# Cutting the first heads' weight products into three spans of rows, with four heads ahead and a rearranged opening

## The chip, the cores and the metric

One Trainium2 chip, one core of it. The metric is the device time of one execution in microseconds (us), as the median of the runs shown; lower is better. Each kernel also has one profiled execution, and the trace that is read below is that one's. TensorE (PE) multiplies, VectorE (DVE), ScalarE (ACT) and GpSimd (POOL) work element by element, SyncE's queue (SP) issues the loads.

## The reference, cut to what matters

Two layers on 256 tokens of 2048 channels, in float32. Each layer has a token mixer and a SwiGLU block; in front of each stands a norm whose scale and shift come from a conditioning vector `c`.

```python
c_act = silu(c)
for i in range(2):
    sh1, sc1, g1, sh2, sc2, g2 = split(c_act @ w_mod[i] + b_mod[i], 6)
    h = rms_norm(x, norm1_g[i]) * (1 + sc1) + sh1
    y = retention_mixer(h, cos, sin, ...) if i == 0 else short_conv_mixer(h, ...)
    x = x + g1 * y
    h = rms_norm(x, norm2_g[i]) * (1 + sc2) + sh2
    x = x + g2 * swiglu(h, ...)
return rms_norm(x, final_g)
```

The retention mixer has eight heads. Each needs, of `h @ w_in`, 256 columns of queries, 256 of keys, 512 of values and 512 of gates. Queries and keys are turned by an angle (position times a frequency, through sine and cosine), their scores are weighted by a decay, multiplied with the values, normed, and multiplied with silu of the gates.

## The kernel before, in words

**Layout.** `x` is kept transposed: 16 rows (tiles) of 128 channels x 256 tokens. A *unit* is the product of one 128 x 128 block of weights with one row. To keep float32's precision, weights and rows are each split into a high part and the rest (`hi`, `lo`; `h[k][:, 0]`, `h[k][:, 1]`), and a unit is three matmuls of 256 columns (`packed`, L348 to L366: hi x high at L361, hi x low at L362, lo x high at L363) or one of 512 and one of 256 (`product`, L328, lines L338 and L341).

**Weights.** All weights lie in one array in the order of use (`in_use_order`, `laid_out`), in blocks of 1 MB, one load each. `prepare` (L282) takes half of such a block (128 x 1024, eight units): ACT casts the high part (L295), DVE subtracts it from the raw weights (L296). `take` (L301) hands out the next unit's weights, and prepares when none is ready; from `early` units on it holds `AHEAD` = 2 more halves ready.

**Modulation.** Scale, shift and gate are made one column of 128 channels at a time (`modulation`, L232): a load of 1 MB of `w_mod`, one DVE instruction that multiplies 128 x 2048 with silu of `c` and sums (L238), and one or two operations on a column on POOL (L243, L245, L248). Those of the first norm are made in the opening, all others beside later products, at points that `plan_mod` (L257) gives in units done; the first are due from `early` - 64 = 376 units on.

**Opening.** Loads of `c`, `x`, the columns and a table (frequencies and identity) are issued first (L194 to L222). The 16 squares go to ACT one by one, DVE adds them (L384 to L388), PE sums the one tile over partitions (L396), DVE makes the mean (L405), POOL the root (L407), PE spreads it (L414) and ACT copies it to `rb` (L577). Then `row(k)` makes row k of `h`: DVE multiplies x with the scale and `rb` (`u`, L424), ACT adds the shift for the high part (L431), DVE makes the low part (L432). Each row needs two modulation columns first.

**First heads.** The products of heads 0 and 1 (queries, keys, gates: 16 columns in eight PSUM banks, all that there are) run row by row as the rows are made, for rows 0 to 10 (`RET_FIRST`, `FIRST_KS` = 11; L592). The banks are copied to SBUF (`held`, L565) as `ahead`. Then the angles are worked out (L595, L529 to L561: 19 operations on DVE, two sines on ACT). Then rows 0 to 10 of heads 2, 3 and 4 are multiplied pair by pair of columns (`RET_SECOND`, L598 to L603), while rows 11 to 15 are made. After that the heads come one by one (`projections`, L714): `pair` (L704) multiplies the five late rows for heads 0 to 4 and adds what was held (L711), `rope` turns queries and keys, `values` (L627; L634 to L636) multiplies all 16 rows, `scores` (L646; first matmul L656, split at L378), two more `pair`s for the gates, and the rest of the head (`mixed`, L670) is done in steps among later products (`asides`, `STEPS`). 460 units stand ahead of head 0's values: 16 x 11 + 24 x 11, and 2 x 2 x 5 for its queries and keys.

**Order.** PE runs in the order in which the program is written (`manual_schedule`, L188), through the whole kernel. DVE and ACT are in written order only within the opening (L588); elsewhere the framework's scheduler orders them. Tile pools set when a buffer comes free: three raw tiles for the weights, three for the opening's modulations (`START_RAWS`), four high and four low parts.

Of the kernel before, what the change touches and what calls it, by code (L numbers as in the profile page):

```python
# [33 lines left out]
FIRST_KS = 11  # L34
EARLY_HEADS = 5
START_RAWS = 3
# [19 lines left out]
class Group:  # L56
    """Output columns of a matrix that are worked out together, in the order of their rows."""
# [29 lines left out]
def out_groups(rows, parts, tail, lead):  # L87
    """The first columns' products with the last rows, which are made last, come after the others."""
# [21 lines left out]
RET_FIRST, RET_SECOND, RET_HEADS = ret_in_groups()  # L110
# [7 lines left out]
def in_use_order():  # L118
    """Each group of the weights, with its matrix and the matrix's index, in the order of use."""
    yield "ret_w_in", 0, RET_FIRST  # L120
    for groups in RET_SECOND:
        for g in groups:
            yield "ret_w_in", 0, g
# [19 lines left out]
def laid_out(arrays):  # L143
    """The weights in the order of their use, as blocks of 128 rows and CHUNK columns."""
# [27 lines left out]
def trunk(ctx: ExitStack, tc: tile.TileContext, x_in, c_in, pos_in, w_mod, cols_in, tab_in, w_all, out):  # L172
# [21 lines left out]
    with tc.tile_pool(name="crow", bufs=1) as cp:  # L194
        row = cp.tile([1, D], F32, tag="row", name="row")
        nc.sync.dma_start(row, c_in)
        for i in range(0, D, 2 * S):
            pt = ps.tile([P, 2, S], F32, tag="bank", name=name("bank")).rearrange("p a b -> p (a b)")
            nc.tensor.matmul(pt, ones[0:1, :], row[:, i : i + 2 * S], start=True, stop=True)
            nc.scalar.activation(cb[:, i : i + 2 * S], pt, AF.Silu)  # L200
    x = []
    for i in range(0, KT, 4):
        t = const.tile([P, 4, S], F32, tag=f"x{i}", name=f"x{i}")
        nc.sync.dma_start(t, x_in[:, i : i + 4, :])
        x += [t[:, j, :] for j in range(4)]
    n_cols = cols_in.shape[1]
    cols = const.tile([P, n_cols], F32, tag="cols", name="cols")
    nc.sync.dma_start(cols, cols_in)
# [13 lines left out]
    nc.sync.dma_start(tab, tab_in[:, : 1 + P])  # L222
# [9 lines left out]
    def modulation(layer, which, j, pool=wpool, bufs=RAW_BUFS):  # L232
        t = layer * 6 * KT + which * KT + j
        raw = pool.tile([P, CHUNK], F32, tag="raw", name=name("raw"), bufs=bufs)
        nc.sync.dma_start(raw, w_mod[t])
        total = tmp("msum", (P, 1), bufs=4)
# [289 lines left out]
    with ExitStack() as inner:  # L526
# [322 lines left out]
```

## Time and profile before

| | us |
|---|---|
| runs: lowest, median, highest of 3 | 2663.68, 2667.03, 2669.86 |
| profiled execution, span from first to last instruction | 2660.6 |
| PE busy in the span | 2621.9 |
| DVE, ACT, POOL busy in the span | 2017.8, 1248.4, 214.0 |
| PE busy from 0 to 31 / 31 to 104 / 104 to 120 / 120 to 211 | 14.1 / 63.7 / 15.5 / 91.0 |
| DVE busy in the same four stretches | 18.8 / 72.8 / 15.9 / 65.4 |
| mean rate of loads and stores over the span | 258 GB/s |

Rows of the trace in time order give the start and the duration (us), the engine, the line, the operation, what is written and read, and the shape; in brackets stands how long the engine waited before and for what. PEld is PE's loading of weights, SPq the issue of a load on SP's queue. Rows of the waits give the waiting instruction, what ended the wait, the sum, the number and the longest. Rows of windows give for a stretch the busy time and count of PE, PEld, DVE, ACT and POOL, then the granted TensorE clock (1.00 is full), the load engines' busy share and GB/s. Rows of groups give busy time and mean ns of one, then the idle time before them and what ended it. "x4" at the end of a row counts the instructions that it stands for.

### The profile page before, as it was taken

What the parts mean: (1) busy time and instruction counts of PE and PEld (TensorE: products, weight loads), DVE (VectorE), ACT (ScalarE), POOL (GpSimd) and SP (SyncE); (2) the same over time, 40 slices, a digit from 0 to 9 for tenths busy, and PEclk for the clock granted to TensorE, in tenths of its full rate; (3) what the DMA queues carried; (4) which work ended last, traced back from release to release, by engine and by line L of the source; (5) the groups of instructions that cost most, each with busy time, mean ns of one, the idle gap of its engine ahead of it and who ended that gap; (6) DMA issues with size and microseconds to landing.
All of it is one profiled execution on the core that took longest, in us unless ns stands there. A gap on an engine that the chain in (4) does not pass through costs nothing.

```text
span 2660.6 us, 40134 instructions
## 1 busy us (share of the span) xinstructions
PE 2621.9 (99%) x16044; PEld 2335.6 (88%) x16044; DVE 2017.8 (76%) x2655; ACT 1248.4 (47%) x1782; POOL 214.0 (8%) x278
## 2 busy tenths in 40 slices
PE   6999999999999999999999999999999999999998
PEld 5898988999989888888888898888998888888887
DVE  8968988887698877777777889878887665555554
ACT  3444543444456444334444454444554443444443
POOL 4310000011000010100000001100000000000000
PEclk9999999999999999999999999999999999999999
DMA  9976667777677877777777768776777765555553
GB/s 374 400 265 242 251 217 296 267 270 263 250 267 261 312 281 267 298 271 284 285 268 282 268 219 321 287 282 256 268 269 256 264 220 190 185 185 189 189 190 127
DMA packets 96957, 687.69 MB, mean 258 GB/s; under 512 B 10753, under 2 KB 12545, under 8 KB 13825
## 3 DMA queue, kind: packets, MB, share of 16 engines
q1 hardware_dynamic: 96770, 685.13, 69.3%
q8 instruction: 125, 2.05, 0.3%
q14 instruction: 62, 0.51, 0.1%
HBM read 682.99 MB, written 2.10 MB: 257 GB/s over the span
## 4 chain that ended last, share of the span: by engine, by line
PE 76%; issue 19%; DVE 3%; DMA 0%; POOL 0%; ACT 0%; DVEq 0%; ACTq 0%; POOLq 0%
PE bank L338 35%; PE bank L341 18%; PE bank L363 4%; PE bank L361 4%; PE bank L362 4%; PE bank L634 2%; PE bank L635 2%; PE bank L636 2%; PE bank L477 1%; PE bank L476 1%; PE bank L478 1%; DVE raw L238 1%; DVE lo L296 1%; PE bank L680 0%; DMA raw<-w_mod 0%
## 5 line engine op out<-in xcount | busy, mean ns | idle before, releaser
L296 DVE TENSOR_TENSOR lo<-raw,hi 128x1024 fp32r<-128x1024 f32 x912 | 1113.5, 1223 | 561.1 <-ACT hi L295 559.2
L295 ACT CAST hi<-raw 128x1024 fp32r<-128x1024 f32 x912 | 953.9, 1050 | 1087.3 <-PE bank L338 638.5
L338 PE MATMUL bank<-h,hi 128*128 128x512 f32 x3296 | 1155.2, 395 | 0.0
L341 PE MATMUL bank<-h,lo 128*128 128x256 f32 x3296 | 925.5, 281 | 0.0
L338 PEld LDWEIGHTS bank<-h,hi 128*128 128x128 f32 x3296 | 622.7, 189 | 144.9
L338 PE MATMUL bank<-mid,hi 128*128 128x512 f32 x2100 | 731.1, 395 | 0.1
L341 PEld LDWEIGHTS bank<-h,lo 128*128 128x128 f32 x3296 | 623.3, 189 | 0.0
L341 PE MATMUL bank<-mid,lo 128*128 128x256 f32 x2100 | 583.8, 278 | 0.0
L338 PEld LDWEIGHTS bank<-mid,hi 128*128 128x128 f32 x2100 | 394.1, 188 | 92.2 <-DVE mid L378 0.4
L238 DVE SCALAR_TENSOR_TENSOR raw<-raw,cb 128x2048 f32<-128x2048 f32 x192 | 438.5, 2284 | 5.0 <-DMA raw<-w_mod 4.8
L341 PEld LDWEIGHTS bank<-mid,lo 128*128 128x128 f32 x2100 | 395.0, 188 | 0.0
L363 PE MATMUL bank<-h,lo 128*128 128x256 f32 x1024 | 292.4, 286 | 10.0 <-DVE lo L296 10.0
L361 PE MATMUL bank<-h,hi 128*128 128x256 f32 x1024 | 290.6, 284 | 2.8 <-ACT hi L295 2.8
L362 PE MATMUL bank<-h,hi 128*128 128x256 f32 x1024 | 290.3, 284 | 0.6 <-DVE h L432 0.5
L363 PEld LDWEIGHTS bank<-h,lo 128*128 128x128 f32 x1024 | 193.8, 189 | 14.4 <-DVE lo L296 14.4
L361 PEld LDWEIGHTS bank<-h,hi 128*128 128x128 f32 x1024 | 195.7, 191 | 3.5 <-ACT hi L295 3.3
L362 PEld LDWEIGHTS bank<-h,hi 128*128 128x128 f32 x1024 | 193.9, 189 | 2.3 <-DVE h L432 2.3
L243 POOL TENSOR_SCALAR mcol<-msum,cols 128x1 f32<-128x1 f32 x64 | 63.6, 994 | 549.6 <-DVE raw L238 549.6
L634 PE MATMUL bank<-hi,h 128*128 128x512 f32 x256 | 101.4, 396 | 0.0
L635 PE MATMUL bank<-lo,h 128*128 128x512 f32 x256 | 101.0, 395 | 0.0
L636 PE MATMUL bank<-hi,h 128*128 128x512 f32 x256 | 101.0, 394 | 0.0
L370 ACT COPY low<-bank 128x256 f32<-128x256 f32 x254 | 90.7, 364 | 11.7 <-PE bank L341 9.0
(122 smaller groups left out, 1811.6 us busy)
## 6 DMA issues: line engine op xcount, KB each, us to landing
raw<-w_all SPq DMA_DIRECT2D x456, 1024.0 KB, 4.9
raw<-w_mod SPq DMA_DIRECT2D x192, 1024.0 KB, 5.0
x<-x_in SPq DMA_DIRECT2D x4, 512.0 KB, 5.7
out<-out SPq DMA_DIRECT2D x5, 256.0 KB, 2.9
decay<-tab_in SPq DMA_DIRECT2D x8, 128.0 KB, 3.0
out<-out SPq DMA_DIRECT2D x3, 128.0 KB, 2.3
out<-out SPq DMA_DIRECT2D x1, 384.0 KB, 2.7
cols<-cols_in SPq DMA_DIRECT2D x1, 160.0 KB, 7.2
```

Of the source, the lines that this page charges most:

```text
L238: nc.vector.scalar_tensor_tensor(raw, raw, 1.0, cb, op0=ALU.mult, op1=ALU.mult, accum_out=total)
L295: nc.scalar.copy(hi, raw)
L296: nc.vector.tensor_tensor(lo, raw, hi.bitcast(F32), op=ALU.subtract)
L338: nc.tensor.matmul(pt, hi, h, start=fresh and k == g.ks[0], stop=False, skip_group_check=True)
L341: nc.tensor.matmul(pt[:, 1, :], lo, h[:, 0, :], start=False, stop=last and k == g.ks[-1], skip_group_check=True)
L361: nc.tensor.matmul(pt, hi, h[:, 0, :], start=first, stop=False, skip_group_check=True)
L362: nc.tensor.matmul(pt, hi, h[:, 1, :], start=False, stop=False, skip_group_check=True)
L363: nc.tensor.matmul(pt, lo, h[:, 0, :], start=False, stop=last, skip_group_check=True)
L370: nc.scalar.copy(low[:, at], pt[:, 1, at])
L634: nc.tensor.matmul(o, ht[:, 0, :], hi, start=k == 0, stop=False)
L635: nc.tensor.matmul(o, ht[:, 0, :], lo, start=False, stop=False)
L636: nc.tensor.matmul(o, ht[:, 1, :], hi, start=False, stop=k == KT - 1)
```

## The change

- The first heads' products are cut into `SPANS`: heads 0 and 1 with rows 0 to 4, heads 2 and 3 with rows 0 to 8, heads 0 and 1 with rows 5 to 15, each on eight banks row by row. `held` copies a bank the first time and adds it (DVE) the second. Heads 0 and 1 then have no products of queries, keys and gates left (`pair` returns what is held), heads 2 and 3 have rows 9 to 15, heads 4 to 7 all 16. 400 units stand ahead of head 0's values: 80 + 144 + 176.
- Rows 5 to 15 are made during the second and third span, one per 1.7 rows of products (`more`, `ROW_STEPS`), in the scheduler's order; rows 0 to 4 in written order.
- Weights are held `AHEAD` from the end of the first span on, two halves are prepared in front of the first copies, and raw weights are loaded ahead (`fetch`). Later modulations are due from 400 units on.
- The opening is written in order on DVE and ACT: the angles first on DVE (after the positions' load, which is issued behind `x`, the columns and the table), squares in pairs of tiles on ACT (128 x 512), four adds on DVE, sums over eight tiles on PE, the mean on ACT; the sines on ACT are written behind the second span.
- A row's columns are made on ACT (`column`) instead of POOL. DVE multiplies two rows of `x` with `rb` at once (`norm_two`), ACT makes the row twice from it (as float32 and as the high part), DVE subtracts. Four raw tiles for the opening's modulations instead of three.

What is computed is the same. The diff, without empty lines and comments, cut where only names change:

```diff
-FIRST_KS = 11
-EARLY_HEADS = 5
-START_RAWS = 3
+SPANS = (((0, 1), (0, 5)), ((2, 3), (0, 9)), ((0, 1), (5, 16)))
+ROW_STEPS = 1.7
+START_RAWS = 4
...
-    early, late = range(FIRST_KS), range(FIRST_KS, KT)
-    ahead, heads = [], []
+    qkg, v = [], []
...
-        v = Group([V0 + h * DV], DV)
-        if h < EARLY_HEADS:
-            ahead.append([q, k, g[:2], g[2:]])
-            qkg = [Group(c, ks=late) for c in ahead[-1]]
-        else:
-            qkg = [Group(c) for c in (q, k, g[:2], g[2:])]
-        heads.append((qkg, v))
-    first = Group([c for pairs in ahead[:2] for pair in pairs for c in pair], ks=early)
-    second = [[Group(c, ks=early) for c in pairs] for pairs in ahead[2:]]
-    return first, second, heads
+        qkg.append([q, k, g[:2], g[2:]])
+        v.append(Group([V0 + h * DV], DV))
+    done = [0] * HEADS
+    spans = []
+    for heads, (a, b) in SPANS:
+        assert all(done[h] == a for h in heads)
+        for h in heads:
+            done[h] = b
+        spans.append(Group([c for h in heads for pair in qkg[h] for c in pair], ks=range(a, b)))
+    rest = [[Group(c, ks=range(done[h], KT)) for c in qkg[h]] for h in range(HEADS)]
+    return spans, list(zip(rest, v))
...
-    early = 8 * EARLY_HEADS * FIRST_KS
-    plan_mod = [(early - MOD_LEAD, 0), (1024, 18), (1984, 49), (5184, 9 * KT), (5888, n_mod)]
+    first = len(RET_SPANS[0].cols) * FIRST_KS
+    early = sum(len(g.cols) * len(g.ks) for g in RET_SPANS)
+    plan_mod = [(early, 0), (1024, 18), (1984, 49), (5184, 9 * KT), (5888, n_mod)]
...
+    def fetch():
+        raw = wpool.tile([P, CHUNK], F32, tag="raw", name=name("raw"), bufs=RAW_BUFS)
+        nc.sync.dma_start(raw, w_all[n_fetched[0]])
+        n_fetched[0] += 1
+        fetched.append(raw)
...
+            if not fetched:
+                fetch()
+            if first <= units[0] < early and not fetched:
+                fetch()
...
-            while len(ready) < 1 + AHEAD * (units[0] >= early):
+            while len(ready) < 1 + AHEAD * (units[0] >= first):
...
+            pos = sp.tile([P, S], I32, tag="pos", name="pos")
...
-                    r2 = tmp("sum", bufs=4)
-                    nc.vector.scalar_tensor_tensor(r2, k, -part, r, op0=ALU.mult, op1=ALU.add)
-                    r = r2
+                    nc.vector.scalar_tensor_tensor(dst, k, -part, r, op0=ALU.mult, op1=ALU.add)
+                    r = dst
...
-                nc.scalar.activation(dst, r, AF.Sin)
-            return sin, cos
...
-        def held(head, i, pt):
-            n = 4 * head + i
-            tag = f"mid{n}" if n < 2 * HEADS else f"ahead{n}"
-            t = rm.tile([P, 2, S], F32, tag=tag, name=name("ahead"))
-            nc.scalar.copy(t, pt)
-            ahead[head, i] = t
+        def held(n, pt):
+            key = divmod(n, 4)
+            if key in ahead:
+                nc.vector.tensor_tensor(ahead[key], ahead[key], pt, op=ALU.add)
+            else:
+                ahead[key] = rm.tile([P, 2, S], F32, tag=f"mid{n}", name=name("ahead"))
+                nc.scalar.copy(ahead[key], pt)
         with tc.tile_pool(name="start", bufs=1) as sp:
-            acc = None
-            for j in range(KT):
-                acc = squares(acc, x[j])
-            rb = tmp("rb", pool=sp, bufs=1)
-            nc.scalar.copy(rb, rstd([acc], D))
-            def scale(which, k):
+            raws_of, totals = {}, {}
+            def loaded(which, k):
                 if k < KT:
-                    modulation(0, which, k, sp, START_RAWS)
+                    raws_of[which, k] = mod_raw(which * KT + k, sp, START_RAWS)
+            def reduced(which, k):
+                if k < KT:
+                    raw = raws_of.pop((which, k))
+                    total = totals[which, k] = tmp("msum", (P, 1), bufs=4)
+                    nc.vector.scalar_tensor_tensor(raw, raw, 1.0, cb, op0=ALU.mult, op1=ALU.mult, accum_out=total)
+            def column(which, k):
+                dst = (mod_a if which == SC1 else mod_s)[0][0][:, k : k + 1]
+                if which == SC1:
+                    scale, bias = gain[0][0][:, k : k + 1], gain_1[:, k : k + 1]
+                else:
+                    scale, bias = 1.0, b_mod[:, which * KT + k : which * KT + k + 1]
+                nc.scalar.activation(dst, totals.pop((which, k)), AF.Identity, bias=bias, scale=scale)
+                return dst
+            normed_x = {}
+            def norm_two(i):
+                t = normed_x[i] = sp.tile([P, 2, S], F32, tag="two", name=name("two"), bufs=2)
+                both = x4[i // 2][:, 2 * (i % 2) : 2 * (i % 2) + 2, :]
+                nc.vector.tensor_tensor(t, both, rb.unsqueeze(1).to_broadcast([P, 2, S]), op=ALU.mult)
             def row(k):
-                u = scaled(k, rb, 0, 0)
-                scale(SC1, k + 1)
-                shifted(h[k], u, k, 0, 0)
+                a, b = column(SC1, k), column(SH1, k)
+                t = normed_x[k // 2][:, k % 2, :]
+                full = tmp("u", bufs=3)
+                nc.scalar.activation(full, t, AF.Identity, bias=b, scale=a)
+                nc.scalar.activation(h[k][:, 0, :], t, AF.Identity, bias=b, scale=a)
+                return lambda: nc.vector.tensor_tensor(
+                    h[k][:, 1, :], full, h[k][:, 0, :].bitcast(F32), op=ALU.subtract
+                )
+            def both_reduced(k):
+                reduced(SC1, k + 1)
+                reduced(SH1, k + 1)
+                if k % 2 == 0 and k + 2 < KT:
+                    norm_two(k // 2 + 1)
+                ahead_of(k + 2)
+            def ahead_of(k):
+                loaded(SC1, k)
+                loaded(SH1, k)
+                if k < FIRST_KS:
+                    fetch()
             with tc.manual_schedule(engines={mybir.EngineType.DVE, mybir.EngineType.Activation}):
-                scale(SC1, 0)
-                scale(SH1, 0)
+                c_row = sp.tile([1, D], F32, tag="raw", name=name("raw"), bufs=START_RAWS)
+                nc.sync.dma_start(c_row, c_in)
+                for i in range(4):
+                    nc.sync.dma_start(x4[i], x_in[:, 4 * i : 4 * i + 4, :])
+                nc.sync.dma_start(cols, cols_in)
+                nc.sync.dma_start(tab, tab_in[:, : 1 + P])
+                nc.scalar.activation(half, half, AF.Silu)
+                nc.vector.memset(half, -0.5)
+                eps = const.tile([P, 1], F32, tag="eps", name="eps")
+                nc.vector.memset(eps, EPS)
+                angles()
+                loaded(SC1, 0)
+                loaded(SH1, 0)
+                fetch()
+                ahead_of(1)
+                spread_c = []
+                for i in range(0, D, 2 * S):
+                    pt = bank().rearrange("p a b -> p (a b)")
+                    nc.tensor.matmul(pt, ones[0:1, :], c_row[:, i : i + 2 * S], start=True, stop=True)
+                    spread_c.append(pt)
+                def silu(i):
+                    nc.scalar.activation(cb[:, 2 * S * i : 2 * S * i + 2 * S], spread_c[i], AF.Silu)
+                def square(i):
+                    sq = [rm.tile([P, 2, S], F32, tag=f"mid{2 * i + n}", name=name("sq")) for n in range(2)]
+                    for n in range(2):
+                        nc.scalar.activation(sq[n], x4[i][:, 2 * n : 2 * n + 2, :], AF.Square)
+                    return sq
+                def added(a, b):
+                    for n in range(2):
+                        nc.vector.tensor_tensor(a[n], a[n], b[n], op=ALU.add)
+                a = square(0)
+                b = square(1)
+                added(a, b)
+                silu(0)
+                b = square(2)
+                added(a, b)
+                silu(1)
+                silu(2)
+                c = square(3)
+                silu(3)
+                pt = bank()
+                tiles = [t[:, j, :] for t in a + c for j in range(2)]
+                for i, sq in enumerate(tiles):
+                    for t in range(2):
+                        nc.tensor.matmul(
+                            pt[:, 0, t : t + 1], sq[:, t * P : (t + 1) * P], ones[:, 0:1],
+                            start=i + t == 0, stop=i == len(tiles) - 1, skip_group_check=True,
+                        )
+                gain_1 = const.tile([P, KT], F32, tag="gain1", name="gain1")
+                nc.vector.scalar_tensor_tensor(
+                    gain_1, b_mod[:, SC1 * KT : (SC1 + 1) * KT], 1.0, gain[0][0], op0=ALU.add, op1=ALU.mult
+                )
+                reduced(SC1, 0)
+                reduced(SH1, 0)
+                mean = tmp("rs", (P, 2), bufs=4)
+                nc.scalar.activation(mean, pt[:, 0, 0:2], AF.Identity, bias=eps, scale=1.0 / D)
+                r = tmp("rs", (P, 2), bufs=4)
+                nc.gpsimd.tensor_tensor(r, mean, half, op=ALU.pow)
+                rb = tmp("rb", pool=sp, bufs=1)
+                nc.scalar.copy(rb, norm_spread(r))
+                norm_two(0)
                 banks = [bank() for _ in range(8)]
-                pts = packed(RET_FIRST, h, before=row, between=lambda k: scale(SH1, k + 1), banks=banks)
+                def before(k):
+                    low = []
+                    prepare(lambda: low.append(row(k)))
+                    low[0]()
+                pts = packed(RET_SPANS[0], h, before=before, between=both_reduced, banks=banks)
+                prepare()
+                prepare()
                 for i, pt in enumerate(pts):
-                    held(i // 4, i % 4, pt)
-            sin, cos = angles()
-            late = range(FIRST_KS, KT)
-            n = 4 * len(RET_SECOND)
-            for i in range(n):
-                for k in late[i * len(late) // n : (i + 1) * len(late) // n]:
-                    row(k)
-                    scale(SH1, k + 1)
-                (pt,) = packed(RET_SECOND[i // 4][i % 4], h)
-                held(2 + i // 4, i % 4, pt)
+                    held(i, pt)
+            made, step = [FIRST_KS], [0.0]
+            def more(k=None):
+                while made[0] < KT and step[0] >= (made[0] - FIRST_KS) * ROW_STEPS:
+                    row(made[0])()
+                    both_reduced(made[0])
+                    made[0] += 1
+                step[0] += 0.5
+            pts = packed(RET_SPANS[1], h, before=more, between=more, banks=[bank() for _ in range(8)])
+            for i, pt in enumerate(pts):
+                held(8 + i, pt)
+            for dst in (sin, cos):
+                nc.scalar.activation(dst, dst, AF.Sin)
+            pts = packed(RET_SPANS[2], h, before=more, between=more, banks=[bank() for _ in range(8)])
+            assert made[0] == KT
+            for i, pt in enumerate(pts):
+                held(i, pt)
         mid = [None] * (4 * HEADS // 2)
...
             g = RET_HEADS[head][0][i]
+            if not g.ks:
+                return ahead[head, i]
```

More of the change, by code (lines that the diff above doesn't have):

```diff
@@ L118, in in_use_order @@
 def in_use_order():
[L120 to L123, printed above, removed]
+    for g in RET_SPANS:
+        yield "ret_w_in", 0, g
     for h, (qkg, v) in enumerate(RET_HEADS):
@@ L193, in trunk @@
     cb = const.tile([P, D], F32, tag="cb", name="cb")
[L194 to L205, printed above, removed]
+    x4 = [const.tile([P, 4, S], F32, tag=f"x{i}", name=f"x{i}") for i in range(0, KT, 4)]
+    x = [t[:, j, :] for t in x4 for j in range(4)]
     n_cols = cols_in.shape[1]
     cols = const.tile([P, n_cols], F32, tag="cols", name="cols")
-    nc.sync.dma_start(cols, cols_in)
     at = [0]
@@ L221, in trunk @@
     tab = const.tile([P, 1 + P], F32, tag="tab", name="tab")
-    nc.sync.dma_start(tab, tab_in[:, : 1 + P])
     inv_freq, ident = tab[:, 0:1], tab[:, 1 : 1 + P]
@@ L230, in trunk, with mod_raw, modulation @@
     mod_g = [[const.tile([P, KT], F32, tag=f"g{l}{i}", name=f"g{l}{i}") for i in range(2)] for l in range(DEPTH)]
-    def modulation(layer, which, j, pool=wpool, bufs=RAW_BUFS):
-        t = layer * 6 * KT + which * KT + j
+    def mod_raw(t, pool=wpool, bufs=RAW_BUFS):
         raw = pool.tile([P, CHUNK], F32, tag="raw", name=name("raw"), bufs=bufs)
         nc.sync.dma_start(raw, w_mod[t])
+        return raw
+    def modulation(layer, which, j):
+        t = layer * 6 * KT + which * KT + j
+        raw = mod_raw(t)
         total = tmp("msum", (P, 1), bufs=4)
@@ L279, in trunk, with prepare @@
     n_halves = w_all.shape[0] * CHUNK // HALF
-    ready, taken_cols, raws = [], [0], []
-    def prepare():
+    ready, taken_cols, raws, fetched, n_fetched = [], [0], [], [], [0]
+    def fetch():
[3 more added lines that the diff above has]
+        fetched.append(raw)
+    def prepare(between=None):
         n = prepared[0]
@@ L288, in prepare @@
         if i == 0:
-            raw = wpool.tile([P, CHUNK], F32, tag="raw", name=name("raw"), bufs=RAW_BUFS)
-            nc.sync.dma_start(raw, w_all[n * HALF // CHUNK])
-            raws[:] = [raw]
+            if not fetched:
+                fetch()
+            raws[:] = [fetched.pop(0)]
+            if first <= units[0] < early and not fetched:
+                fetch()
         raw = raws[0][:, i : i + HALF]
@@ L295, in prepare @@
         nc.scalar.copy(hi, raw)
+        if between:
+            between()
         nc.vector.tensor_tensor(lo, raw, hi.bitcast(F32), op=ALU.subtract)
```

12 lines of the change are left out of this document (6 added, 6 removed).

## The prediction, made before the changed kernel was run

> **What bounds the kernel now.** I read the page first, then the waits of TensorE, then windows and the timeline of the first 215 us.
>
> ```profile
> span 2660.6 us, 40134 instructions
> PE 2621.9 (99%) x16044; PEld 2335.6 (88%) x16044; DVE 2017.8 (76%) x2655; ACT 1248.4 (47%) x1782; POOL 214.0 (8%) x278
> ```
> ```profile
> PE bank L363 <- DVE lo L296: 10.0, 21, 0.8
> PE bank L396 <- DVE acc L388: 8.5, 1, 8.5
> PE bank L414 <- POOL rs L407: 3.6, 3, 2.1
> ```
> ```profile
> 120.00:150.00 30.00, 30.00 (x255) 30.00 (x255) 22.53 (x23) 14.84 (x18) 4.17 (x6) 1.00 0.78 310
> ```
> ```profile
> 210.55 0.39 PE L634 MATMUL bank<-hi,h 128*128 128x512 f32 x1
> ```
>
> PE bounds the kernel: its idle time is 38.7 us of 2660.6, and its waits belong to the opening. From 120 to 150 us 255 matmuls of 256 columns start in 30 us, 0.118 us apart. The change reorders products and adds none (460 or 400 units of three such matmuls stand before head 0's values), so its worth is the time lost before head 0's values. Before reaches them, at L634, at 210.55 with 460 units done. After has 400 units there; before has done 400 at 210.55 - 180 x 0.118 = **189.3**. That is the mark to beat.
>
> ```profile
> 25.23 0.58 PE L361 MATMUL bank<-h,hi 128*128 128x256 f32 x1 [2.58 <-ACT hi L295]
> 27.82 0.41 PE L361 MATMUL bank<-h,hi 128*128 128x256 f32 x1
> 28.04 0.41 PE L362 MATMUL bank<-h,hi 128*128 128x256 f32 x1
> ...
> 31.33 0.28 PE L363 MATMUL bank<-h,lo 128*128 128x256 f32 x1
> 31.45 0.28 PE L361 MATMUL bank<-h,hi 128*128 128x256 f32 x1
> ```
> ```profile
> 31.05 2.28 DVE L238 SCALAR_TENSOR_TENSOR raw<-raw,cb 128x2048 f32<-128x2048 f32 x1
> 33.26 0.08 DVE L238 DVE_READ_ACCUMULATOR raw<-raw,cb 128x1 f32 x1
> 33.26 0.48 DVE L432 SCALAR_TENSOR_TENSOR h<-u,s,h 128x256 fp32r<-128x256 f32 x1
> 33.66 1.22 DVE L296 TENSOR_TENSOR lo<-raw,hi 128x1024 fp32r<-128x1024 f32 x1
> 34.79 2.29 DVE L238 SCALAR_TENSOR_TENSOR raw<-raw,cb 128x2048 f32<-128x2048 f32 x1
> ```
> ```profile
> 31.23 0.51 ACT L431 ACTIVATE h<-u,s 128x256 fp32r<-128x256 f32 x1 [5.11 <-DVE u L424]
> ...
> 99.04 0.51 ACT L431 ACTIVATE h<-u,s 128x256 fp32r<-128x256 f32 x1 [4.37 <-DVE u L424]
> ```
>
> PE's first weights product starts at 25.23; it runs without breaks from 27.8, first 0.21 apart, from 31.3 on 0.12. Then rows bind: nine rows take 99.04 - 31.23, **7.5 us each**, against 48 x 0.12 = 5.7 of PE. DVE fills them: two reductions at 2.21, two low parts at 1.14, two operations at 0.40.
>
> **The change part by part.** The instruction order built from the changed source fixes what stands behind what; durations are rows of before.
>
> *The start.* DVE's hand-written order now opens with the angles, which wait for positions; their load is issued behind x, cols and tab.
>
> ```profile
> 3.67 0.45 SPq L222 DMA_DIRECT2D tab<-tab_in  x1
> ```
> ```profile
> tab<-tab_in SPq DMA_DIRECT2D x1, 64.5 KB, 6.6
> ```
> ```profile
> 105.96 0.28 DVE L533 CAST acc<-u 128x256 f32<-128x256 int32 x1
> 106.28 0.35 DVE L534 TENSOR_SCALAR acc<-acc,tab 128x256 f32<-128x256 f32 x1
> ```
> ```profile
> L711 DVE TENSOR_TENSOR qs<-ahead,bank 128x512 f32<-128x512 f32 x20 | 13.6, 681 | 1.7 <-PE bank L363 1.6
> L555 DVE SCALAR_TENSOR_TENSOR sum<-u,sum 128x256 f32<-128x256 f32 x6 | 2.5, 418 | 0.0
> L549 DVE TENSOR_SCALAR u<-acc 128x256 f32<-128x256 f32 x2 | 0.5, 290 | 0.0
> ```
> ```profile
> 18.28 0.93 PEld L396 LDWEIGHTS bank<-ones,acc 128*128 128x128 f32 x4 [10.06 <-DVE acc L388]
> ...
> 2647.99 0.74 PEld L396 LDWEIGHTS bank<-ones,acc 128*128 128x128 f32 x6 [1.00 <-ACT acc L384]
> ```
> ```profile
> 20.35 0.15 DVE L405 TENSOR_SCALAR rs<-bank 128x2 f32<-128x2 f32 x1
> ...
> 22.68 0.37 ACT L577 COPY rb<-bank 128x256 f32<-128x256 f32 x1 [7.09 <-PE bank L414]
> ```
> ```profile
> L295 ACT CAST hi<-raw 128x1024 fp32r<-128x1024 f32 x912 | 953.9, 1050 | 1087.3 <-PE bank L338 638.5 <-DMA raw<-w_all 112.5 <-PE bank L362 100.5
> L431 ACT ACTIVATE h<-u,s 128x256 fp32r<-128x256 f32 x64 | 31.4, 507 | 70.3 <-DVE u L424 57.2 <-POOL s L248 8.8 <-PE bank L478 3.7
> L569 ACT COPY ahead<-bank 128x512 f32<-128x512 f32 x20 | 11.5, 584 | 6.9 <-PE bank L363 6.5
> L491 ACT COPY end<-bank 128x1 f32<-128x1 f32 x18 | 2.2, 146 | 0.0
> ```
>
> tab landed at 3.67 + 6.6 = 10.3; positions right behind it, say 10.6 (10.3 to 11.5). The angles are 0.28 + 0.35 + nine like L549 (0.29) + eight like L555 (0.42) and 18 hand-overs of 0.04, each waiting for the one before: 7.3, to 17.9. The squares (four adds of 128x512, 0.6 apart) end at 20.4; DVE's first two reductions then end at 25.0. PE sums eight tiles instead of one: 16 products, 32 passes (before's two products show as x4), from 19.9. Four passes took 0.93 at the start, six 0.74 at the end: 0.12 to 0.23 a pass; I take 0.20, nearest to the early row less its last pass's overhang: 6.4, to 26.3 (23.8 to 27.3). From mean to rb I take before's 20.35 to 23.05, 2.7: 29.1. Then the doubled norm 0.68 on DVE, beside it the weights' cast 1.05 on ACT, two columns (0.15 to 0.25 each), two rows of 0.5: first product 31.4, low row 31.9. Unbroken PE thus begins at 31.9 instead of 27.8: **+4.1**. POOL's column work goes to ACT, idle there, at 0.4 a row.
>
> *Rows 0 to 4.* DVE per row: 4.42 + 2.28 + one plain 128x256 operation (0.34) + half of 0.6 = 7.34. It is unbroken from 31.8: ten reductions, nine low parts, three doubled norms, four rows, to 67.4; PE's last 22 matmuls end the span at **70.1**. Six DVE-bound rows fewer is the gain: 6 x (7.5 - 5.7) = 10.8.
>
> *Between the spans.* All eight banks are full at 70.1. In the built order, row 6 stands ahead of the next weights: DVE makes row 5's low part and row 6's two reductions (to 72.1); ACT makes row 6's columns and full row, then two casts (0.95 apart), then the first bank's copy: 72.2 + 0.3 + 0.4 + 1.9 + 0.6 = **75.4**. PE stands 5.3 us. After so long a gap I count PE slow again:
>
> ```profile
> 2646.68 0.28 PE L363 MATMUL bank<-mid,lo 128*128 128x256 f32 x1
> ```
> ```profile
> 2649.00:2650.00 1.00, 0.16 (x1) 0.16 (x1) 0.02 (x1) 0.00 (x0) 0.69 (x1) 0.58 0.00 0
> 2650.00:2651.00 1.00, 1.00 (x4) 0.77 (x4) 0.00 (x0) 0.00 (x0) 0.00 (x0) 0.50 0.00 0
> ```
>
> The granted clock fell to 0.50 some 2.5 us behind the last dense matmul. About 3.4 us at 0.21 instead of 0.12 cost 1.5 (0 to 1.5 per gap).
> The Trainium skill, TensorE: Matmul & The Clock Gate (Part 1: The HAM clock gate), says that an idle window of about 3.4 us halves the clock and that it then takes as long a busy one to release it; by that rule this gap may or may not hold a whole window, and the sum without the 1.5 would be 9.3. The clock row above agrees with it.
>
> Span 1 needs 432 x 0.118 = 51.0; DVE and ACT keep ahead: 75.4 + 1.5 + 51.0 = 127.9. At its end ACT's order is: last bank's copy 0.6, row 11's column and full row 0.7, then the cast 1.05, then DVE's low part 1.22: PE runs again at **131.5** (+3.5). In span 2 the rows 12 to 14 stand in DVE's order with each low row right behind its reductions, so DVE waits for ACT (two columns, two rows: 1.4) and then for a cast (0.7). From the first weights to the eleventh row's weights DVE needs 12 low parts 13.6, six reductions 13.3, rows 1.9, waits 6.2 less what overlaps at the ends (2.1) = 32.9, PE's five rows 28.3: PE gets there at 164.4, and 286 matmuls end at **198.1**. This is 8.8 behind the mark.
>
> *The heads.* Heads 0 and 1 have no q, k or gate products left, so only 12 value or 24 packed matmuls (2.8 us) lie between scores and outputs; before had 60 packed and more.
>
> ```profile
> 232.84 0.39 PE L656 MATMUL bank<-q,k 128*128 128x512 f32 x1
> ```
> ```profile
> 239.05 0.29 DVE L378 TENSOR_TENSOR sp<-sum,sp 128x128 fp32r<-128x128 f32 x1
> ```
>
> From scores to the last split before took 6.5; PE now covers 1.2 + 2.8 = 4.0. Two waits of 0 to 2.5; I take 1.0 each: **+2.0**. Twelve sums fewer and eight more in SBUF save DVE 2.7 and PE nothing, as it does not wait there. Modulations start at 400 units instead of 376, beside PE; loads are the same megabytes.
>
> **Sum:** 8.8 + 2.0 = 10.8: span 2671.4. The runs' median, 2667.03, lies 6.4 above the profiled span (what lies around the span, and run to run); with it **2677.8**.
>
> **Rivals.**
> *Cheap boundaries.* If casts and copies get through while DVE makes row 6, gaps cost one copy each (0.6) and clock and DVE waits vanish: 10.8 - 4.7 - 1.5 - 2.9 - 2.9 = -1.2 us, 2665.8: no change. For it: before left such a boundary at 103 with waits of 0.4 only. Against: after's order on ACT.
> *Faster.* Mechanism: the opening chain on PE and DVE. If rb comes as early as before's (23.05; angles beside the loads, sums at 0.12), unbroken PE starts at 27.8, and with cheap boundaries the time is 2665.8 - 4.1 = 2661.7, at best 2659. It decides at a start below 28 and both gaps under 1 us. For it: PE waits 8.5 for sums now. Against: DVE's order puts 7.3 us of angles first.
> *Slower still.* Each gap halves the clock (1.5 more at two) and heads wait 2.5 each (3 more): 2683.8.
> *It does not do what it says*: were DVE to hold span 1 as well (row 9.8 us of work per 9.6 of PE, without cover), 3 rows x 1.5: 2682.
>
> **How the numbers follow.** A measurement of this kernel tells about 0.2% (5.3 us) from no change. Forecast 0.58 (2671 to 2684: the bounds of the start, 23.8 to 27.3 for the sums, and of the two head waits), slower still or bound in span 1 0.14, cheap boundaries 0.16, faster 0.12. Of the forecast's spread 0.01 lies below 2672.3. Faster 0.12, same 0.17, slower 0.71. Range 2664 to 2686, which holds cheap boundaries and leaves out the faster case and the far end of the slow ones.
>
> **What would show it.** First weights product at 31 to 32; L614's first row behind it; rows 7.3 apart on DVE; a PE gap of 5 us near 70 that ends with ACT's first `ahead` copy; a second near 128; head 0's values at 198. Wrong, if PE starts below 29, if the gaps are under 1 us, or if the losses lie behind 200 us.

## The result, and the profile after

The changed kernel takes **2679.98 us** (median of 4 runs, 2678.31 to 2683.71) beside 2668.25 us for the one before (4 runs, 2663.68 to 2669.86): a ratio of 1.0054, 95% interval 1.004 to 1.0068, so slower by 0.5%. Run once more beside the later experiments it took 2680.80 us against 2665.50 (1.0054, interval 1.0042 to 1.0067). Forecast were 2677.8 us, and 10.8 us more than before.

The page of the changed kernel has, of the lines shown of before:

```profile
span 2681.9 us, 40112 instructions
PE 2630.7 (98%) x16072; PEld 2345.5 (87%) x16072; DVE 2012.4 (75%) x2634; ACT 1260.2 (47%) x1819; POOL 153.0 (6%) x230
```

The profiled execution took 2683.71 us, 1.8 us more than its span, and it was the longest of the four; the spans of the other three were 2676.5 to 2679.4. Before's profiled span (2660.6) was a short one, so the 21.3 us between the two spans are more than the change. What the change does is read from the stages ahead of head 0's values.

The waits of TensorE from 0 to 205 us, in the changed kernel (waiting instruction, what ended it, sum, times, longest):

```profile
PE bank L682 <- DVE sq L666: 10.5, 1, 10.5
PE bank L368 <- DVE lo L301: 7.9, 7, 1.7
PE bank L366 <- ACT ahead L575: 5.2, 1, 5.2
PE bank L366 <- ACT hi L298: 3.6, 2, 2.4
PE bank L366 <- ACT h L613: 3.0, 1, 3.0
```

Before had 21 short waits for low parts (10.0) and one of 8.5 for the sums. Now there are seven for low parts, the wait for the sums is 10.5, and single waits of 5.2 and 2.4 stand where before had none. Four places hold them.

**The start.** From the timeline, VectorE's angles and what waits for them:

```profile
11.23 0.29 DVE L539 CAST ang<-pos 128x256 f32<-128x256 int32 x1 [8.89 <-DMA pos<-pos_in]
18.34 2.49 DVE L666 TENSOR_TENSOR sq<-sq,sq 128x512 f32<-128x512 f32 x4
20.28 6.99 PE L682 MATMUL bank<-ones,sq 128*128 128x1 f32 x32 [10.48 <-DVE sq L666]
29.65 0.37 ACT L697 COPY rb<-bank 128x256 f32<-128x256 f32 x1 [2.08 <-PE bank L419]
32.62 0.58 PE L366 MATMUL bank<-h,hi 128*128 128x256 f32 x1 [3.00 <-ACT h L613]
```

VectorE does nothing for 8.9 us until the positions are there, then the angles until 18.3, then the adds; TensorE sums for 7 us more. The first weights product comes at 32.62 instead of 25.23.

**The boundary behind heads 0 and 1's first rows.** What ends TensorE's 5.2 us, from the timelines of VectorE, ScalarE and TensorE:

```profile
68.76 2.30 DVE L588 SCALAR_TENSOR_TENSOR raw<-raw,cb 128x2048 f32<-128x2048 f32 x1
70.97 2.30 DVE L588 SCALAR_TENSOR_TENSOR raw<-raw,cb 128x2048 f32<-128x2048 f32 x1
73.32 0.29 ACT L597 ACTIVATE s<-msum,cols 128x1 f32<-128x1 f32 x1 [1.82 <-DVE raw L588]
74.15 1.97 ACT L298 CAST hi<-raw 128x1024 fp32r<-128x1024 f32 x2
76.03 3.49 ACT L575 COPY ahead<-bank 128x512 f32<-128x512 f32 x7
76.66 0.58 PE L366 MATMUL bank<-h,hi 128*128 128x256 f32 x1 [5.19 <-ACT ahead L575]
```

ScalarE waits for row 6's second reduction until 73.3, although row 6 is not multiplied for another 30 us; the casts and the copies that empty the banks stand behind it in its order.

**The clock.** Windows around the first and the second boundary (last three columns: granted clock, load engines' share, GB/s):

```profile
71.00:75.00 4.00, 0.46 (x4) 0.26 (x3) 2.89 (x5) 2.04 (x4) 0.00 (x0) 1.00 1.02 426
75.00:76.00 1.00, 0.00 (x0) 0.00 (x0) 0.79 (x1) 1.00 (x2) 0.00 (x0) 0.65 1.04 434
76.00:82.00 6.00, 5.34 (x25) 5.34 (x26) 4.79 (x5) 6.00 (x12) 0.00 (x0) 0.50 0.74 294
...
133.00:134.00 1.00, 0.42 (x2) 0.21 (x2) 1.00 (x1) 1.00 (x2) 0.00 (x0) 0.67 0.00 0
134.00:140.00 6.00, 5.82 (x27) 5.82 (x28) 6.00 (x7) 2.20 (x3) 0.00 (x0) 0.50 0.58 213
140.00:141.00 1.00, 1.00 (x10) 1.00 (x10) 1.00 (x3) 0.29 (x1) 0.00 (x0) 0.92 0.97 410
```

After each boundary some 25 matmuls start 0.21 us apart instead of 0.12: about 2.3 and 2.6 us.

**The second boundary, and head 0.** The end of the gap behind the second span, and head 0's first values product:

```profile
132.92 0.39 PE L366 MATMUL bank<-h,hi 128*128 128x256 f32 x1 [2.43 <-ACT hi L298]
134.18 0.58 PE L368 MATMUL bank<-h,lo 128*128 128x256 f32 x1 [0.76 <-DVE lo L301]
...
201.97 0.39 PE L762 MATMUL bank<-hi,h 128*128 128x512 f32 x1
```

Head 0's values begin at 201.97, which is 12.7 us behind the mark of 189.3. From 205 to 345 us the heads add these waits, where before had 0.4 in all:

```profile
PE bank L808 <- DVE sp L383: 2.2, 2, 1.1
PE bank L419 <- POOL rs L412: 1.6, 2, 1.4
```

### The profile page after: what moved, and what is told of

It reads as the page before. It is cut to its first block, busy times and chain, and to the rows that moved or that the text cites. A ratio compares the mean times of both kernels' runs of the same rounds, so it can differ in the third digit from the quotient of the medians.

```text
span 2681.9 us, 40112 instructions
## 1 busy us (share of the span) xinstructions
PE 2630.7 (98%) x16072; PEld 2345.5 (87%) x16072; DVE 2012.4 (75%) x2634; ACT 1260.2 (47%) x1819; POOL 153.0 (6%) x230
## 4 chain that ended last, share of the span: by engine, by line
PE 71%; issue 21%; DVE 5%; DMA 2%; ACT 1%; POOL 0%; DVEq 0%; ACTq 0%; POOLq 0%
PE bank L343 33%; PE bank L346 17%; PE bank L368 4%; PE bank L366 4%; PE bank L367 4%; PE bank L762 2%; PE bank L764 2%; PE bank L763 2%; PE bank L482 1%; DVE lo L301 1%; PE bank L481 1%; DMA raw<-w_all 1%; PE bank L483 1%; DVE raw L588 1%; ACT hi L298 1%
## 5 line engine op out<-in xcount | busy, mean ns | idle before, releaser
L232 DVE SCALAR_TENSOR_TENSOR raw<-raw,cb 128x2048 f32<-128x2048 f32 x160 | 365.6, 2285 | 14.4 <-DMA raw<-w_mod 14.1
L366 PEld LDWEIGHTS bank<-h,hi 128*128 128x128 f32 x1024 | 198.2, 194 | 12.7 <-ACT ahead L575 5.4
L242 POOL TENSOR_TENSOR g<-msum,cols 128x1 f32<-128x1 f32 x64 | 34.3, 535 | 910.6 <-DVE raw L232 910.6
```

Source lines behind the costliest of these rows:

```text
L232: nc.vector.scalar_tensor_tensor(raw, raw, 1.0, cb, op0=ALU.mult, op1=ALU.mult, accum_out=total)
L366: nc.tensor.matmul(pt, hi, h[:, 0, :], start=first, stop=False, skip_group_check=True)
```

## The experiments

The theory: the change loses at four places (the angles ahead of the sums; the order at the first boundary; the same at the second; two heads with too little between scores and outputs), each an order of work and not an amount. The rivals: VectorE, ScalarE or the loads are full, so that what is saved at one place comes back at another; or the cut into three spans is itself the loss. Line numbers differ by some lines between these kernels.

### e1_angles_late

```diff
-                angles()
                 loaded(SC1, 0)
...
+            angles()
             made, step = [FIRST_KS], [0.0]
```

> The changed kernel, but the 19 operations for the angles (and the load of positions) stand behind the first span instead of first in VectorE's order. My theory: they delay the squares' sums by about 7 us, and with that the first weights product, which comes at 24.5 us here instead of 32.6 us; the second span has some 8 us of free VectorE time, so most of the 7.3 us are hidden there, and the gap at the first boundary stays (5 us, granted clock 0.5 behind it): 2673 us, against 2680.0 for the changed kernel. Rival (VectorE's work is only moved, and the rows pay it back): first product at 24.5 us, but head 0's values no earlier than 201 us: 2679 us. Second rival (the start waits for loads, not for the angles): first product still behind 30 us, 2680 us.

Measured: **2671.22 us** (ratio to before 1.0018, interval 1.0009 to 1.0027), 8.8 us below the changed kernel.

```profile
7.22 1.29 DVE L665 TENSOR_TENSOR sq<-sq,sq 128x512 f32<-128x512 f32 x2 [4.87 <-ACT sq L660]
...
22.18 0.58 PE L366 MATMUL bank<-h,hi 128*128 128x256 f32 x1 [3.00 <-ACT h L613]
...
192.49 0.39 PE L762 MATMUL bank<-hi,h 128*128 128x512 f32 x1
```

The start comes 10.4 us earlier, 3 us ahead of before's 25.23, and 9.5 of that still stand at head 0's values. It is more than the angles' 7 us because the adds no longer wait for the positions either: they begin at 7.22 instead of 18.34. The angles themselves are hidden in the second span. The gap at the first boundary (5.2 us) is the same as before. Both rivals fall.

### e2_written_order

The `with tc.manual_schedule(...)` of the opening covers the second and third span too (the lines from `made, step = ...` to the last `held` are indented); nothing else differs.

> The changed kernel, but VectorE and ScalarE keep the written order through the second and the third span as well, so that at each boundary the casts and the copies of the banks stand ahead of the next rows' work. My theory (order, not amount of work, makes the gaps): the gap behind the first span falls from 5.5 us to under 1 us, the one behind the second from 2.7 us and 1 us to under 1 us, the granted clock stays at 1.00 through both (2.3 and 2.6 us saved), the stall at the eleventh row's weights goes; a new VectorE wait of 2 us may come in the second span: 2668 us, head 0's values at 190 us. Rival (VectorE and ScalarE have too much work, gaps come back elsewhere): 2678 to 2682 us. Second rival (clock falls anyway): 2673 us.

Measured: **2671.77 us** (1.002, interval 1.0011 to 1.0028), 8.2 us below the changed kernel, 3.8 us above the expectation. Head 0's values begin at 192.60. No gap is left at 71 us, at the second boundary or at the eleventh row's weights. The granted clock stays at 1.00 through both boundaries. A new gap stands at 78 us; VectorE's timeline and TensorE's row:

```profile
76.53 0.43 DVE L614 TENSOR_TENSOR h<-u,h 128x256 fp32r<-128x256 f32 x1 [4.07 <-ACT h L613]
76.88 2.28 DVE L588 SCALAR_TENSOR_TENSOR raw<-raw,cb 128x2048 f32<-128x2048 f32 x1
...
82.58 0.58 PE L368 MATMUL bank<-h,lo 128*128 128x256 f32 x1 [4.58 <-DVE lo L301]
```

VectorE waits 4.1 us for row 5, which ScalarE makes behind its eight copies, and then has two reductions ahead of the weights' low part. It is again an order, and the wait was expected as 2 us, not 4.6; the clock is at 0.50 behind it, from 79.8 to 86.6 us.

### e3_old_spans and e10_changed_three_raws

```diff
-SPANS = (((0, 1), (0, 5)), ((2, 3), (0, 9)), ((0, 1), (5, 16)))
+SPANS = (((0, 1), (0, 11)), ((2, 3), (0, 11)), ((4,), (0, 11)))
-START_RAWS = 4
+START_RAWS = 3
...
-            pts = packed(RET_SPANS[2], ..., banks=[bank() for _ in range(8)])
+            pts = packed(RET_SPANS[2], ..., banks=[bank() for _ in range(4)])
...
-                held(i, pt)
+                held(16 + i, pt)
```

The second kernel has only the `START_RAWS` line.

> The new opening with spans like those of before: heads 0 and 1, heads 2 and 3, head 4, each with rows 0 to 10; three raw tiles in the opening instead of four, for room. My theory (the start costs 5 us, the order at the boundary 5 us and the half clock 2 us, whatever the length of the spans; the heads' waits of 4 us come only with whole spans): first product at 32.6 us, a gap of some 5 us at 113 us, no waits between scores and outputs: 2677 us. Rival (the short spans are the whole loss): 2670 us. Second rival (the spans as such gain nothing and lose nothing): 2680 us.

> The changed kernel with three raw tiles in the opening instead of four, alone. It tells how much of e3_old_spans' time is its third tile. My theory (from e8 against e5: 6.4 us): reductions wait for loads in the later rows: 2684 us, so that three spans against the old ones gain 5 us where both have three raw tiles. Rival (with the later start of this opening the loads have slack): 2680 us, and the spans gain nothing measurable here.

Measured: **2679.18 us** for the old spans (1.0049, interval 1.0036 to 1.0063) and **2681.62 us** for the changed kernel with three raw tiles (1.0056, 1.0041 to 1.0071). The old spans under the new opening are as slow as the change: the first rival of e3 falls, the second holds, and so does e10's rival. With three raw tiles each, the cut into spans makes no difference that the intervals show. By the trace it still moves time: head 0's values begin at 226.17 with 460 units, so 400 units were done at 226.17 - 180 x 0.118 = 205.0, against 201.06 with the three spans; the heads' waits (5.5 us in e10, none with the old spans) then take these 4 us back. Head 0's first values product of e3 and of e10, and the waits of e3, which has the boundary too:

```profile
226.17 0.39 PE L762 MATMUL bank<-hi,h 128*128 128x512 f32 x1
```
```profile
201.06 0.39 PE L762 MATMUL bank<-hi,h 128*128 128x512 f32 x1
```
```profile
PE bank L368 <- DVE lo L301: 13.8, 9, 2.4
...
PE bank L366 <- ACT ahead L575: 5.2, 1, 5.2
```

### e4_later_outputs

```diff
-            return list(zip(STEPS, [lambda: outputs(0), ...
+            steps = (24,) + STEPS[1:] if head < 2 else STEPS
+            return list(zip(steps, [lambda: outputs(0), ...
```

> The changed kernel, but heads 0 and 1 begin their outputs 24 units behind the scores instead of 8 (the first of the four steps alone). My theory: the two waits of 1.0 and 1.1 us at the first outputs go, and the roots' waits of 1.4 and 0.2 us stay: 2677.8 us. Rival (what follows is late instead: roots and the next head): 2680.0 us.

Measured: **2676.61 us** (1.004, interval 1.0027 to 1.0052), 3.4 us below the changed kernel. From 205 to 345 us the only wait left is

```profile
PE bank L419 <- POOL rs L412: 1.5, 1, 1.5
```

against 3.8 in the changed kernel: the waits at the outputs are gone, and one of the two for the roots with them. But in this execution the half clock also lasted less long, 3.4 us instead of 6.8 behind both boundaries, and head 0's values, which the edit does not touch, begin at 200.24 instead of 201.97. So 1.7 us of this profiled execution's lead come from ahead of the edit, and how much of the 3.4 between the medians is the edit's is not shown.

### e5_together, e7_together_old_spans and e8_three_raws

Written order as in e2; row making starts one row of products later; `angles` yields after each operation, and the sines stand behind the third span's products.

```diff
-                angles()
...
-            made, step = [FIRST_KS], [0.0]
+                made, step, turn = [FIRST_KS], [-1.0], angles()
...
+                    if step[0] > 6.0:
+                        next(turn, None)
```

e7 is this with e3's spans and three raw tiles, e8 with the three raw tiles alone.

> Written order through all three spans (as in e2_written_order), rows 5 to 15 begun one row of products later, and the angles neither first nor in one piece: one of their 19 operations per half row, from the fifth row of the second span on. My theory: start as in e1_angles_late (first product 22.2 us, 10 us earlier), no gap at either boundary, and no VectorE wait like the 4.9 us that e2_written_order had at 78 us, since ScalarE's copies are done before the first row's sums are wanted: head 0's values at 176 to 181 us instead of 202, 2656 us, below before's 2666.4. Rival (VectorE is full: eleven rows, 40 low parts and the angles are some 112 us of its time in the 113 us of both spans): values at 188 us, 2665 us.

> e5_together with the spans of e3_old_spans (rows 0 to 10 of heads 0 and 1, of 2 and 3, of 4; three raw tiles in the opening). My theory: five more... six more rows at 7.5 us instead of 5.7 us beside the products cost about 10.8 us, the heads' waits of 3.7 us go: 2663 us, that is 7 us more than e5_together. Rival (the spans themselves gain nothing): 2655 us, no more than e5_together.

> e5_together with three raw tiles in the opening instead of four, alone. My theory: the rows of the first span are bound by VectorE, loads have some slack: 0 to 2 us more than e5_together, 2657 us. Rival (three raw tiles delay the reductions in all sixteen rows, about 0.4 us a row as in e3_old_spans): 2662 us.

Measured: **2660.24 us** for e5 (0.9977, interval 0.9969 to 0.9986: below before), **2667.87** for e7 (1.0014, 1.0005 to 1.0023), **2666.68** for e8 (1.001, 1.0001 to 1.0019). e5 lies between its two theories: head 0's values begin at 182.99, 19 us earlier than in the changed kernel and not 21 to 26. e7 came out 7.6 us above e5, as expected, but for another reason: one raw tile less costs 6.4 us here by itself, the amount of e8's rival and not of its theory (0 to 2), and the spans gain 1.2 us, which the intervals do not tell from nothing. The 6.4 are not 0.4 in every row: the last wait of the first span ends only 0.3 us later (58.51 against 58.18), and the rest comes with a longer gap and half clock at the first boundary and a wait for a low part near 130 us (4.2 instead of 2.1). So it is the fourth raw tile, not the spans, that carries e5 below e7; in the changed kernel, where the start is 10 us later, the same tile is worth nothing measurable (2681.62 against 2680.80). One thing is not shown: the old spans were run with three raw tiles for room. They hold 20 copies of banks (128 x 512 each) where the three spans hold 16, and four such copies are as large as one raw tile (128 x 2048). The cut may so have its worth as the room for the fourth tile; the old spans with four were not run. Head 0's first values product in e5, e7 and e8:

```profile
182.99 0.39 PE L773 MATMUL bank<-hi,h 128*128 128x512 f32 x1
```
```profile
215.33 0.39 PE L773 MATMUL bank<-hi,h 128*128 128x512 f32 x1
```
```profile
188.71 0.39 PE L773 MATMUL bank<-hi,h 128*128 128x512 f32 x1
```

### e6_together_outputs and e9_weights_first

e6 is e5 with e4's line. e9 is e6 with

```diff
                 loaded(SH1, k)
-                if k < FIRST_KS:
+                if k < FIRST_KS + 1:
                     fetch()
```

> e5_together with heads 0 and 1 beginning their outputs 24 units behind the scores instead of 8. My theory: 3.4 us less than e5_together, as e4_later_outputs gained over the changed kernel: 2652.5 us. Rival (with an earlier start the modulations of later stages are due beside the heads at another point and VectorE is late there): the same as e5_together, 2656 us.

> e6_together_outputs, but the load of the second span's first weights is issued one row earlier, ahead of the loads for row 6's modulation columns. My theory (in e5 and e6 the gap of 2.7 us at 61 us is a cast that waits for a load, and that load stands behind two loads of 1 MB that nobody needs yet, with all 16 load engines busy): the gap falls below 0.7 us and the granted clock stays at 1.00 (1.2 us more): 2653 us. Rival (the loads as a whole are late, and what is put ahead only delays the next rows): a new wait of VectorE or TensorE of 3 us before 130 us, 2656.8 us as e6.

Measured: **2656.76 us** for e6 (0.9971, interval 0.9959 to 0.9982) and **2653.03 us** for e9 (0.9953, 0.9941 to 0.9966). e6 lies 3.5 us below e5, the gain that its theory took from e4, though the profiled executions show only 0.8 us less of TensorE's waits from 176 to 420 us (2.8 against 3.6). In e6 a window in the first span and the cast behind it, then the same cast in e9:

```profile
50.00:60.00 10.00, 8.06 (x65) 7.86 (x66) 7.83 (x9) 1.98 (x3) 0.00 (x0) 1.00 1.01 416
```
```profile
60.91 1.99 ACT L299 CAST hi<-raw 128x1024 fp32r<-128x1024 f32 x2 [8.93 <-DMA raw<-w_all]
```
```profile
56.81 1.99 ACT L299 CAST hi<-raw 128x1024 fp32r<-128x1024 f32 x2 [4.73 <-DMA raw<-w_all]
58.71 3.99 ACT L584 COPY ahead<-bank 128x512 f32<-128x512 f32 x8
```

With the early start the loads run at 416 GB/s with all engines busy, and the cast waited for a load that stood behind 2 MB for row 6. Issued ahead of them, it comes 4.1 us earlier, the gap of 2.7 us at the boundary is gone, and 3.7 us of the total with it: the expectation (2653) holds. What comes back is small, a wait of 1.1 us for a low part at 73 us. This kernel is 0.47% faster than before and 1.0% faster than the change.

## Why the prediction held, point by point

**Sign, size and place were right.** 10.8 us were forecast, 8.8 ahead of head 0's values and 2.0 in the heads; the ratio 1.0054 gives 14.4 us on 2667 (10.7 to 18.1 by its interval, so the forecast lies at its lower end). The profiled executions give 12.7 and 3.8. Of the sum's 6.4 us for "what lies around the span, and run to run", 1.8 lie around it; the rest was before's short profile.

**The start: right, 1.2 us too early.** Forecast were angles to 17.9, adds to 20.4, sums 6.4, first product 31.4, unbroken 31.9 (+4.1). Measured: 18.3, 20.8, 7.0, 32.6, and 33.1 for the first product with a low row (+5.3). The positions landed at 11.2 instead of 10.6, and a pass took 0.218 us, not 0.20. e1 shows that the angles are the cause. Rows 0 to 4 then came 7.3 us apart, as forecast.

**The first boundary: right in cause and size.** Forecast 70.1 to 75.4, ended by the first copy; measured 71.4 to 76.7, ended by it. e2 shows the cause: with the casts and copies ahead, the gap goes. The clock's term was mis-sized, 1.5 against 2.3 us. The row from which it was read shows a fall 2.5 us behind the last dense matmul, with other work of TensorE at 2647.99 in between; that is not the whole idle window of the rule that the prediction sets beside it, so the row does not agree with that rule, though the prediction says it does.

**The second boundary: the gap was right, the clock was left out.** Forecast was a restart 3.5 us late; measured are 2.4 and 0.8 us of waits. The sum counted no half clock there, and the range at most 1.5 a gap; it cost 2.6. Most of that took the place of the next term: TensorE came later to the eleventh row's weights, and the stall there was 1.9 us instead of 32.9 - 28.3 = 4.6. That the two nearly cancel was luck: the clock was not in the sum. Head 0's values were forecast 8.8 us behind the mark and came 12.7 behind it. Of the 3.9 us, 1.3 had come up by the first boundary (the start), 1.2 in the second span (the clock), and 1.4 from there on.

**The heads: right for the outputs, short for the roots.** Two waits of 1.0 were forecast, 1.03 and 1.15 measured; 1.6 us of waits for the roots of heads 1 and 2 were not foreseen.

**The gain of 10.8 us from fewer rows bound by VectorE is the term that the experiments correct.** With equal raw tiles the three spans are 3.9 us (e10 against e3) or, from 215.33 - 21.2 = 194.1 to 188.7, 5.4 us (e8 against e7) earlier at head 0's values, and nothing measurable in the total. In the prediction's own terms that would be six rows' gain, less the second boundary with its clock and stall (3.2, 2.6 and 1.9 us), less the heads' waits; no run takes these apart. So it is the angles at the head of the opening and the first boundary, which e3 has as well, that make the change slower, and not the cut.

**The rivals.** "Cheap boundaries" needed gaps of one copy (0.6 us), "faster" gaps under 1 us and a start below 28 too. e9 is a kernel in which both hold, and it beats before by 12.5 us, while 2661.7 was forecast for that case: its start lies at 22, not 27.8, and its outputs begin later. The mechanism of that rival was right; ScalarE's and VectorE's orders decided against it. "DVE holds span 1" did not occur: in the second span of the changed kernel TensorE ran without a wait. In "slower still" the first gap's 1.5 us, already in the sum, seem to be counted again: 2677.8 with 1.5 for the second gap and 3 for the heads is 2682.3, not 2683.8.

What stays open: the changed kernel's profiled executions differ by some us behind 345 us (spans of 2681.9 and 2679.2 with head 0's values at 201.97 and 202.34). TensorE's waits there are 3.2 and 3.1 us, so the difference is not one of waits; what it is stays open. A wait of 1.8 us for a low part at 125 us remains in e9.

## What to carry to other kernels

At a boundary where all banks change hands, look at each engine's order and not at its load: here a reduction for a row wanted 30 us later stood ahead of the copies, and cost 5 us and the clock behind it. Ask the same of a queue of loads once it is full: 1 MB wanted now behind 2 MB wanted later cost 4 us. And test the halves of a change that regroups work and rearranges its opening separately; here the regrouping was neutral in the total with three raw tiles on both sides, and the angles' place in the opening and the order at the boundaries were what cost.

## What the runs showed of the hardware that was not expected

The granted clock fell behind shorter waits than the prediction had counted on. In e3_old_spans, around a single wait of 1.9 us (66.9 to 68.8), the windows show:

```profile
66.00:67.00 1.00, 0.89 (x8) 0.68 (x6) 1.00 (x3) 0.00 (x0) 0.00 (x0) 1.00 1.01 418
67.00:68.00 1.00, 0.00 (x0) 0.00 (x0) 1.00 (x2) 0.39 (x1) 0.00 (x0) 1.00 1.03 426
68.00:69.00 1.00, 0.23 (x1) 0.23 (x2) 1.00 (x2) 1.00 (x3) 0.00 (x0) 0.97 1.01 418
69.00:70.00 1.00, 1.00 (x6) 1.00 (x6) 0.91 (x1) 0.97 (x3) 0.00 (x0) 0.50 1.02 426
```

TensorE was already at work again when the clock halved, for 3.4 us. The waits of 1.7 us in the first span of the changed kernel had no such effect, and nor had two of 2.0 us in this same run (97.9 to 99.9 and 112.9 to 114.9): the length of a wait alone does not decide. One of 2.4 us (82.3 to 84.7) halved it 1.3 us after its end:

```profile
85.00:86.00 1.00, 1.00 (x10) 1.00 (x10) 1.00 (x2) 1.00 (x2) 0.00 (x0) 1.00 1.05 434
86.00:87.00 1.00, 1.00 (x7) 1.00 (x6) 1.00 (x2) 0.16 (x1) 0.00 (x0) 0.50 1.01 418
```

Read in windows of 0.2 us, the clock of this run fell at 68.9, 86.0 and 120.1 us and rose at 72.4, 89.4 and 127.0; in the changed kernel it fell at 75.3 and 133.3 and rose at 82.1 and 140.2. Within each run these times lie whole multiples of 3.41 us apart (from 68.9 to 86.0 it is five, from 75.3 to 133.3 seventeen), and each half clock lasts one or two of them. In the 3.41 us ahead of the three falls of e3 TensorE had been idle for 55, 62 and 68% of the time; at 99.7 and 116.7 us, two more such points, for 51 and 48%, and the clock stayed at 1.00. So in these runs the clock seems to be set at fixed points 3.41 us apart, by whether TensorE was idle for more than about half of the stretch before, and a wait of 1.9 or 2.0 us halves it or not, as it lies between the points. That holds for stretches of 256-column matmuls: in before, with one-column products of 0.8 us at 2648 us, the clock fell at 2649.2 us after idle times of 37%.

The Trainium skill, TensorE: Matmul & The Clock Gate (Part 1: The HAM clock gate), gives an idle window of about 3.4 us as the condition; these runs show the clock halved after single waits of 1.9 and 2.4 us, so a wait shorter than that window is not safe here. The same section calls the window free-running; the trace agrees: with the same gap of 5.2 us from 71.5 us on, the clock fell at 75.3 us and was back at 82.1 in the changed kernel, and fell at 76.1 and was back at 79.5 in e4_later_outputs.
